# Memory-attention scores as three float32r products in place of one float32 product

## The chip, the cores and the metric

The kernel runs on one core of a Trainium2 chip. The metric is the device time of one execution in microseconds (us), as the median of several runs. Beside it there is one profiled execution, whose trace gives the start and the duration of every instruction on every engine. The engines are called as in the profile: PE (TensorE, matrix products), PEld (its weight loads), DVE (VectorE), ACT (ScalarE), POOL (GpSimd) and SP (SyncE, which here only issues transfers).

## The reference: what is computed

Two layers of an encoder for 256 tokens of width 2048. Each layer makes one wide projection of the normed tokens, splits it among three groups of heads, and projects their joint output back. The group that matters here is the memory attention: 4 heads of 128 columns, whose queries come from the projection and whose keys and values come from 256 memory tokens.

```python
h = rmsnorm(x, norm_g[l])
proj = h @ w_in[l]
a_x, a_b, a_c, a_g, d_q, d_k, d_v, d_g, m_q, m_g = jnp.split(proj, offsets, axis=-1)
# ... group A: gated conv -> y_a ; group D: differential attention, 6 heads -> y_d
mk = rmsnorm(mkv[..., :W_MEM].reshape(b, N_MEM, MEM_HEADS, MEM_HEAD_DIM), mem_k_norm_g[l])
mq = rmsnorm(m_q.reshape(b, s, MEM_HEADS, MEM_HEAD_DIM), mem_q_norm_g[l])
sc = jnp.einsum('bshd,bmhd->bhsm', mq, mk).astype(jnp.float32) * (MEM_HEAD_DIM ** -0.5)
p = jax.nn.softmax(sc, axis=-1)
y_m = jnp.einsum('bhsm,bmhd->bshd', p, mv).reshape(b, s, W_MEM) * jax.nn.silu(m_g)
x = x + jnp.concatenate([y_a, y_d, y_m], axis=-1) @ w_out[l]
```

The change touches the line `sc = ...`, for 4 heads in each of 2 layers: 8 score matrices of 256 queries by 256 memory tokens.

## The kernel before, in words

**Products.** The large projections are made in float32r: every operand `v` is split into a high part `hi` (a copy into a float32r tile, on ACT) and a low part `lo = v - hi` (on DVE), and a product is the sum of three: high by high, high by low, low by high. Lines 301 to 303 are those three, each with a 128x128 stationary operand and 512 moving columns. The weights come from memory in pieces, are split by lines 280 (`hi`) and 281 (`lo`), and each of the tiles `raw`, `hi` and `lo` has four buffers. The scores of the differential heads (lines 541 and 542) are float32r as well, with 256 moving columns. The memory heads' scores (line 587) are one plain float32 product for each 128 queries: `mqT` by `mkT`, two float32 tiles.

**Chunks.** The function `block` walks over the 16 row tiles of a weight matrix two at a time. One such pair is a chunk: it loads and splits the weights, issues 12 products of 512 columns (2 row tiles, 2 token tiles, 3 products), and then calls `run_side`, which advances the side work. Side work is written as Python generators in the list `tasks`: each runs until its next `yield n`, and is due again `n` chunks later. So the order of the program is written by the chunk counter. A block of the projections is 8 chunks.

**A pair of heads.** The generator `pair` takes two heads through scores, softmax, transposes, the weighted sum with the values (line 434, `po`), the output gate, another transpose, and the split of the result into `yT`. Each turn of a matrix goes out to memory and back by eight transfers on the SP queue, four out (line 413) and four back (line 417), two chunks later (`carry`). At most two pairs' `e` tiles are held at once (`held["e"]`). Count the chunks of a layer from the end of the block in which `start` is set (block 4 of the projection), and the memory heads stand like this before the change: the turned queries are issued at chunk 31 and put the layer into `queries`; heads 0 and 1 are scored at 31 and 33, heads 2 and 3 at 39 and 41; the weighted sums stand at 47, 49, 55 and 57, the outward transfers of the outputs at 61 and 69, and the outputs are split into `yT` (lines 252 and 253) at 63, 64, 71 and 72. The output projection begins with chunk 73 and takes the row tiles of the heads first: those of memory heads 2 and 3 (row tiles 14 and 15) in chunk 77.

**What fixes the order.** Instructions wrapped in `keep_in_program_order` (`pin`) stay in the order of the program on their engine. The others, among them lines 280 and 281, all products of the blocks and everything in `mem_scores`, are placed by the planner of the framework, which simulates the program when it is built. Each engine then works through its own list.

**Slots.** `yT` has 32 slots of 128x256 (2 parts by 16 row tiles) per layer. Row tiles 0 to 5 are the conv groups, 6 to 11 the differential heads, 12 to 15 the memory heads. Until the outputs come, the slots are used otherwise: slots 0 to 5 of both parts hold the differential queries, 6 to 11 the first form of the keys, and 12 to 15 (`k_second`) the second form of the keys of differential heads 0 to 3. The set `scored` holds the differential heads whose scores have been issued.

Of the kernel before, what the change touches and what calls it, by code (L numbers as in the profile page):

```python
# [11 lines left out]
F32 = mybir.dt.float32  # L12
F32R = mybir.dt.float32r
I32 = mybir.dt.int32
AF = mybir.ActivationFunctionType
ALU = mybir.AluOpType
# [3 lines left out]
P = 128  # L20
D_MODEL = 2048
SEQ = 256
# [6 lines left out]
CG = W_CONV // P  # L29
DH = W_DIFF // P  # L30
# [18 lines left out]
def encoder(ctx: ExitStack, tc: tile.TileContext, x, mem, norm_g, w_in, conv_w, conv_b,  # L49
            dq_g, dk_g, lq1, lk1, lq2, lk2, head_g, mem_norm_g, w_mem_kv, mq_g, mk_g, w_out, out):  # L50
    nc = tc.nc
    x, mem, out = x[0], mem[0], out[0]

    def pool(name, bufs, space=None):
        kw = {"space": space} if space is not None else {}
        return ctx.enter_context(tc.tile_pool(name=name, bufs=bufs, **kw))
# [6 lines left out]
    small = pool("small", 3)  # L63
# [7 lines left out]
    def nm(s):  # L71
        uid[0] += 1
        return f"{s}_{uid[0]}"
# [131 lines left out]
    def later(g, n):  # L205
        due[id(g)] = chunk[0] + n
        return g
# [200 lines left out]
    def carry(sheet, to):  # L408


        d = dram.tile([NA, B, NA, sheet.shape[-1]], F32, name=nm("d"))
        for a in range(NA):
            tc.keep_in_program_order(nc.sync.dma_start(d[:, :, a].rearrange("b c r -> c b r"), sheet[a * B:(a + 1) * B]))
        yield 2
        of = d.rearrange("b c a (n i) -> (b c) a n i", i=B)
        for a in range(NA):
            tc.keep_in_program_order(nc.sync.dma_start(to[:, :, a], of[:, a]))
# [11 lines left out]
    def weighted(eT, i, v, h):  # L429

        po = ps_t.tile([P, NT, P], F32, tag="t", name=nm("po"))
        for t in range(NT):
            for k in range(NT):
                nc.tensor.matmul(po[:, t, :], eT[:, i, t, k, :], v[:, k, h * P:(h + 1) * P],  # L434
                                 start=k == 0, stop=k == NT - 1)
        return po
# [52 lines left out]
    scored = set()  # L489
# [3 lines left out]
    def pair(heads, begin, end, v):  # L493

        es = []
        for h in heads:
            while held["e"] == 2:
                yield 1
            held["e"] += 1
            es.append((yield from begin(h)))  # L500
            yield 2
        yield 4
        while held["sh"] == 2:
            yield 1
        held["sh"] += 1
        sh = tmp.tile([P, NA, 2, NT * NT, B], F32, tag="sh", name=nm("sh"))
        for i, e in enumerate(es):
            tc.keep_in_program_order(nc.vector.transpose(
                sh[:, :, i], e[0].rearrange("p t (k b c) -> p b (t k) c", k=NT, b=NA)))
            held["e"] -= 1  # L510
            yield 1
        yield 4
        flat = sh.rearrange("p b h n c -> p (b h n c)")
        yield from carry(sh.rearrange("p b h n c -> p b (h n c)"), flat.rearrange("p (n a i) -> p n a i", a=NA, i=B))
        eT = flat.rearrange("p (h t k q) -> p h t k q", h=2, t=NT, k=NT)
        while held["yn"] == 2:
            yield 1
        held["yn"] += 1
        yn = tmp.tile([P, NA, 2, NT, B], F32, tag="yn", name=nm("yn"))
        for i, h in enumerate(heads):  # L520
            end[0](h, yn[:, :, i], weighted(eT, i, v, h), *es[i][1:])
            yield 2
        held["sh"] -= 1
        yield 5
        tc.keep_in_program_order(nc.vector.transpose(yn, yn))
        yield 5
        flat = yn.rearrange("p b h t c -> p (b h t c)")
        yield from carry(yn.rearrange("p b h t c -> p b (h t c)"), flat.rearrange("p (n a i) -> p n a i", a=NA, i=B))
        for i, h in enumerate(heads):
            end[1](h, flat[:, i * SEQ:(i + 1) * SEQ])  # L530
            yield 1
        held["yn"] -= 1
# [45 lines left out]

    queries = set()

    def mem_scores(l, h, qT, kT, st):
        while l not in queries:
            yield 1
        sc = P ** -0.5
        s = ps_s.tile([P, NT, SEQ], F32, tag="s", name=nm("s"))
        for i in range(NT):
            nc.tensor.matmul(s[:, i, :], qT[:, h, i * P:(i + 1) * P], kT[:, h, :], start=True, stop=True)  # L587
        mx = small.tile([P, NT], F32, tag="mmx", name=nm("mmx"))
        nc.vector.tensor_reduce(mx, s, AX.X, ALU.max)
        nc.vector.tensor_scalar(mx, mx, -sc, None, ALU.mult)  # L590
        sm = small.tile([P, NT], F32, tag="msm", name=nm("msm"))
        e = tmp.tile([P, NT, SEQ], F32, tag="e", name=nm("me"))
        for i in range(NT):
            nc.scalar.activation(e[:, i], s[:, i], AF.Exp, bias=mx[:, i:i + 1], scale=sc, accum_out=sm[:, i:i + 1])
        r = small.tile([P, NT], F32, tag="mr", name=nm("mr"), bufs=6)
        nc.vector.reciprocal(r, sm)
        nc.vector.tensor_tensor(r, r, st[:, HR], ALU.mult)
        return e, r

    def mem_out(h, yn, po, r, a):  # L600
        for i in range(NT):
            nc.vector.scalar_tensor_tensor(yn[:, :, i], strips(po[:, i, :]), r[:, i:i + 1],
                                           strips(a[:, i, h * P:(h + 1) * P]), ALU.mult, ALU.mult)
# [25 lines left out]
    def stats_of(parts, tag):  # L629
        ss = small.tile([P, NT], F32, tag="ssum", name=nm("ssum"))  # L630
        nc.vector.tensor_reduce(ss, parts, AX.X, ALU.add)
        return row_stats(ss, tag)

    def T_tile(what):
        kept.append(big.tile([P, 2, KT, SEQ], F32R, tag="T", name=nm(what)))
        return kept[-1]
# [52 lines left out]
    mkT, mv, away, raws, parts = [], [], [], {}, {}  # L689
# [96 lines left out]
    for _ in range(DEPTH):  # L786
        l = len(mkT)
# [38 lines left out]
    for g in range(3, NG):  # L826
        l, k = divmod(g, KT)
# [19 lines left out]
    for l in range(DEPTH):  # L847
        st = stats_of(ssx, "st")
# [5 lines left out]
        yT = T_tile("yT")  # L854
# [5 lines left out]
        def begin_pair(n, p):  # L860
            tasks.append(later(p, max(1, start + PAIR_EVERY * n - chunk[0])))
# [4 lines left out]
        for b in order:  # L866
# [7 lines left out]
            if b == 4:  # L874
                start = chunk[0]
# [18 lines left out]
        mqT = keep.tile([P, MH, SEQ], F32, tag="mqT", name=nm("mqT"))  # L894
# [13 lines left out]
            split_T(yT, CG + DH + h, y, None, pin=True)  # L908

        for n in range(MH // 2):  # L910
            begin_pair(DH // 2 + n, pair((2 * n, 2 * n + 1), lambda h: mem_scores(l, h, mqT, mkT[l], st),
                                         (lambda h, yn, po, r: mem_out(h, yn, po, r, mga), mem_done), mv[l]))


# [80 lines left out]
        for b in range(4):  # L995
# [3 lines left out]
            for t in range(NT):  # L999
                n = 256 if final else NB  # L1000
# [41 lines left out]
```

## Time and profile before

| | |
|---|---|
| time, median of 3 runs | 924.3 us (923.94 to 925.61) |
| profiled execution, its own time | 924.17 us |
| its span, first to last instruction | 922.4 us |
| PE busy | 917.4 us, 99% of the span, 4176 products |
| DVE busy | 669.9 us, 73% |
| ACT busy | 495.0 us, 54% |
| transfers | 215.06 MB, 233 GB/s over the span |
| granted clock of PE | 1.00 |

The span is shorter than the time: some work lies ahead of the first and behind the last instruction. A product in the trace overlaps the next one, so its own duration (379 ns for line 587) is not what it costs; the cost is read from the chain of waits, which lists what each product adds to the time (its pitch). A float32 product of the program is shown as two records: line 587 has 16 products in the program and 32 records.

### The profile page before, as it was taken

How to read it: one execution, taken by the hardware profiler on the slowest of the kernel's cores; microseconds unless marked ns; L12 is line 12 of the kernel's file. 1: busy time of each engine (PE TensorE's matmuls, PEld its weight loads, DVE VectorE, ACT ScalarE, POOL GpSimd, SP SyncE). 2: the span in 40 equal slices, each digit the busy share in tenths (PEclk: the TensorE clock that was granted, in tenths of full speed). 3: DMA queues.
4: the chain of work that ended last, by engine and by line, in shares of the span. 5: the costliest groups of instructions: out<-in, count | busy, mean ns of one | idle time of the engine just before them, and what ended most of it. 6: DMA issues, size and time to landing. Idle time of an engine off the chain costs nothing.

```text
span 922.4 us, 12254 instructions
## 1 busy us (share of the span) xinstructions
PE 917.4 (99%) x4176; PEld 760.6 (82%) x4176; DVE 669.9 (73%) x1179; ACT 495.0 (54%) x754; POOL 7.0 (1%) x18
## 2 busy tenths in 40 slices
PE   9999999999999999999999999999999999999998
PEld 6888888888888888888888888888888888888886
DVE  5797777857898786567676757878898776558652
ACT  6676545675545554445455544568554554446431
POOL 0001000000000000000000000000000000000000
PEclk9999999999999999999999999999999999999999
DMA  8998778876779999988687867886889889988662
GB/s 277 275 275 299 248 229 234 258 206 198 182 214 252 226 267 249 271 244 243 215 264 233 247 188 225 236 236 179 239 229 236 256 213 260 242 239 240 210 220 73
DMA packets 250226, 215.06 MB, mean 233 GB/s; under 512 B 131166, under 2 KB 176820, under 8 KB 250164
## 3 DMA queue, kind: packets, MB, share of 16 engines
q1 hardware_dynamic: 248004, 210.72, 80.0%
q0 software_dynamic: 672, 2.10, 0.6%
q10 hardware_dynamic: 1488, 1.46, 0.5%
q8 instruction: 33, 0.54, 0.2%
q14 instruction: 29, 0.24, 0.1%
HBM read 193.26 MB, written 20.97 MB: 232 GB/s over the span
## 4 chain that ended last, share of the span: by engine, by line
PE 98%; DMA 1%; SPq 0%; DVE 0%; ACT 0%; issue 0%; DVEq 0%
PE acc L301 28%; PE acc L303 28%; PE acc L302 28%; PE acc L735 9%; PE po L434 2%; PE s L587 1%; DMA raw<-in_w_mem_kv_dram 1%; PE s L542 1%; PE s L541 1%; PE pt L713 0%; SPq L699 0%; SPq L693 0%; DVE lo L708 0%; ACT hi L707 0%; DVE xs L1003 0%
## 5 line engine op out<-in xcount | busy, mean ns | idle before, releaser
L280 ACT CAST hi<-raw 128x1024 fp32r<-128x1024 f32 x288 | 302.8, 1052 | 347.0 <-PE acc L303 298.6
L281 DVE TENSOR_TENSOR lo<-raw,hi 128x1024 fp32r<-128x1024 f32 x288 | 351.9, 1223 | 185.4 <-ACT hi L280 180.4
L301 PE MATMUL acc<-hi,xT 128*128 128x512 f32 x896 | 350.2, 392 | 0.0
L302 PE MATMUL acc<-lo,xT 128*128 128x512 f32 x896 | 349.0, 390 | 0.0
L303 PE MATMUL acc<-hi,xT 128*128 128x512 f32 x896 | 348.8, 389 | 0.0
L303 PEld LDWEIGHTS acc<-hi,xT 128*128 128x128 f32 x896 | 168.2, 188 | 35.0
L301 PEld LDWEIGHTS acc<-hi,xT 128*128 128x128 f32 x896 | 168.2, 188 | 34.0
L302 PEld LDWEIGHTS acc<-lo,xT 128*128 128x128 f32 x896 | 168.3, 188 | 33.8
L301 PE MATMUL acc<-hi,yT 128*128 128x512 f32 x256 | 99.6, 389 | 0.0
L302 PE MATMUL acc<-lo,yT 128*128 128x512 f32 x256 | 99.6, 389 | 0.0
L303 PE MATMUL acc<-hi,yT 128*128 128x512 f32 x256 | 99.6, 389 | 0.0
L735 PE MATMUL acc<-hi,memT 128*128 128x512 f32 (+1 forms) x260 | 72.8, 394 | 0.2
L303 PEld LDWEIGHTS acc<-hi,yT 128*128 128x128 f32 x256 | 48.1, 188 | 10.1
L301 PEld LDWEIGHTS acc<-hi,yT 128*128 128x128 f32 x256 | 48.1, 188 | 9.9
L302 PEld LDWEIGHTS acc<-lo,yT 128*128 128x128 f32 x256 | 48.1, 188 | 9.9
L735 PEld LDWEIGHTS acc<-hi,memT 128*128 128x128 f32 x260 | 47.1, 188 | 10.8 <-ACT hi L707 0.8
L708 DVE SCALAR_TENSOR_TENSOR lo<-raw,cva,hi 128x1024 fp32r<-128x1024 f32 (+2 forms) x37 | 41.7, 1137 | 8.8 <-ACT hi L707 7.9
L707 ACT ACTIVATE hi<-raw,cva 128x1024 fp32r<-128x1024 f32 (+2 forms) x37 | 37.6, 1033 | 9.6 <-DMA raw<-in_w_mem_kv_dram 8.1
L735 PE MATMUL acc<-lo,memT 128*128 128x512 f32 (+1 forms) x130 | 39.9, 388 | 0.0
L735 PEld LDWEIGHTS acc<-lo,memT 128*128 128x128 f32 x130 | 24.3, 188 | 5.2
L552 ACT ACTIVATE e<-e,mx 128x256 f32<-128x256 f32 x48 | 23.8, 499 | 1.4 <-DVE mx L548 1.3
L546 DVE SCALAR_TENSOR_TENSOR e<-dist,s 128x512 f32<-128x512 f32 x24 | 15.7, 681 | 2.3 <-PE s L542 1.9
(147 smaller groups left out, 591.3 us busy)
## 6 DMA issues: line engine op xcount, KB each, us to landing
raw<-in_w_in_dram SPq DMA_DIRECT2D x192, 512.0 KB, 4.4
raw<-in_w_out_dram SPq DMA_DIRECT2D x64, 512.0 KB, 4.2
raw<-in_w_in_dram SPq DMA_DIRECT2D x64, 256.0 KB, 4.6
raw<-in_w_mem_kv_dram SPq DMA_DIRECT2D x30, 512.0 KB, 4.0
d<-sh SPq DMA_DIRECT2D x80, 128.0 KB, 3.9
sh<-d SPq DMA_DIRECT2D x64, 128.0 KB, 4.9
d<-yn SPq DMA_DIRECT2D x40, 64.0 KB, 3.6
yn<-d SPq DMA_DIRECT2D x40, 64.0 KB, 4.2
```

Source lines behind the costliest of these rows:

```text
L280: nc.scalar.copy(hi, raw)
L281: nc.vector.tensor_tensor(lo_, raw, hi.bitcast(F32), ALU.subtract)
L301: nc.tensor.matmul(acc[t], sh, hi, start=first, stop=False)
L302: nc.tensor.matmul(acc[t], sh, lo, start=False, stop=False)
L303: nc.tensor.matmul(acc[t], sl, hi, start=False, stop=last)
L434: nc.tensor.matmul(po[:, t, :], eT[:, i, t, k, :], v[:, k, h * P:(h + 1) * P], start=k == 0, stop=k == NT - 1)
L541: nc.tensor.matmul(s[c][:, i, :], qi, k_first(yT, c, h), start=True, stop=False)
L546: nc.vector.scalar_tensor_tensor(e[:, c], dist, -slopes[h], s[c], ALU.mult, ALU.add)
L552: nc.scalar.activation(e[:, c, i], e[:, c, i], AF.Exp, bias=mx[:, c, i:i + 1], accum_out=sm[:, c, i:i + 1])
L707: pin(nc.scalar.activation(hi, raw, AF.Copy, scale=gain))
L708: pin(nc.vector.scalar_tensor_tensor(lo, raw, gain, hi.bitcast(F32), ALU.mult, ALU.subtract))
L735: pin(nc.tensor.matmul(accs[l, half][t][:, at:at + n], memT[:, token_part, k, t * P:(t + 1) * P], p, start=k == 0 and at == 0 and token_pa ...
```

## The change

For every memory head, query and key are split into a high and a low part, as the other operands are, and the score is the sum of three float32r products of 256 columns. The parts of the key stand in a new tile `mkp` of one buffer; those of the query stand in slots 12 to 15 of `yT`, the ones that the outputs of the same heads take later. Since differential keys stand there before, the scores now wait until all six differential heads are in `scored`. Between the splits and the products there is a `yield 1`.

```diff
-    def mem_scores(l, h, qT, kT, st):
-        while l not in queries:
+    def mem_scores(l, h, yT, qT, kT, st):
+        while l not in queries or not all((l, d) in scored for d in range(DH)):
             yield 1
         sc = P ** -0.5
+        q = yT[:, :, CG + DH + h, :]
+        k = small.tile([P, 2, SEQ], F32R, tag="mkp", name=nm("mkp"), bufs=1)
+        for parts, of in ((k, kT), (q, qT)):
+            nc.scalar.copy(parts[:, 0], of[:, h, :])
+            nc.vector.tensor_tensor(parts[:, 1], of[:, h, :], parts[:, 0].bitcast(F32), ALU.subtract)
+        yield 1
         s = ps_s.tile([P, NT, SEQ], F32, tag="s", name=nm("s"))
         for i in range(NT):
-            nc.tensor.matmul(s[:, i, :], qT[:, h, i * P:(i + 1) * P], kT[:, h, :], start=True, stop=True)
+            for q_part, k_part in ((0, 0), (0, 1), (1, 0)):
+                nc.tensor.matmul(s[:, i, :], q[:, q_part, i * P:(i + 1) * P], k[:, k_part],
+                                 start=q_part + k_part == 0, stop=q_part == 1)
...
-            begin_pair(DH // 2 + n, pair((2 * n, 2 * n + 1), lambda h: mem_scores(l, h, mqT, mkT[l], st),
+            begin_pair(DH // 2 + n, pair((2 * n, 2 * n + 1), lambda h: mem_scores(l, h, yT, mqT, mkT[l], st),
```

## The prediction

> **What bounds the kernel now.** I read the head of the profile page first: the span, the busy time of PE, its slices, the granted clock, and the chain of waits by engine and by line.
>
> ```profile
> span 922.4 us, 12254 instructions
> ...
> PE 917.4 (99%) x4176; PEld 760.6 (82%) x4176; DVE 669.9 (73%) x1179; ACT 495.0 (54%) x754; POOL 7.0 (1%) x18
> ...
> PE   9999999999999999999999999999999999999998
> ...
> PEclk9999999999999999999999999999999999999999
> ...
> PE 98%; DMA 1%; SPq 0%; DVE 0%; ACT 0%; issue 0%; DVEq 0%
> PE acc L301 28%; PE acc L303 28%; PE acc L302 28%; PE acc L735 9%; PE po L434 2%; PE s L587 1%; DMA raw<-in_w_mem_kv_dram 1%; PE s L542 1%; PE s L541 1%; PE pt L713 0%; SPq L699 0%; SPq L693 0%; DVE lo L708 0%; ACT hi L707 0%; DVE xs L1003 0%
> ```
>
> PE sets the end: the chain that ended last is PE for 98% of the span, and PE is busy in every slice at a granted clock of full speed. So whatever PE no longer does comes off the time, and work of the other engines costs nothing until PE has to wait for it. Line 587, the scores that change, is 1% of the chain. PE and PEld have the same count, so every product has its own weight load; nothing is saved by two products in a row with the same stationary operand.
>
> Next I read the pitch of the products from the chain of waits in order of time (start, us added, what). First a stretch of nothing but 512-column products, 31 of them between the two rows; then one memory head of before; then one differential head, whose 8 products of lines 541 and 542 have the shape and type that the change gives to the memory heads.
>
> ```profile
> 416.95 0.23 PE acc L301
> ...
> 423.98 0.23 PE acc L302
> ```
>
> ```profile
> 300.16 0.23 PE acc L303
> 300.39 0.87 PE s L587 x4
> 301.26 0.23 PE acc L301
> ```
>
> ```profile
> 264.02 0.12 PE s L541
> ...
> 264.84 0.12 PE s L542
> 264.96 0.24 PE acc L301
> ```
>
> The 512-column product costs (423.98 - 416.95) / 31 = 0.2268 us. A memory head costs 0.87 us, in four records (two float32 products). The float32r products of 256 columns cost (264.96 - 264.02) / 8 = 0.1175 us each. The groups of PE's instructions, kept apart by shape, show the two shapes and how many records there are of the old one:
>
> ```profile
> L541 PE MATMUL s<-yT 128*128 128x256 f32 x48 | 12.3, 286 | 0.0
> ...
> L587 PE MATMUL s<-mkT,mqT 128*128 128x256 f32 x32 | 8.2, 379 | 0.0
> ```
>
> **PE's part of the change.** Removed: 32 records, four for each of 8 heads, 8 x 0.87 = 6.96 us. Added: 2 x 3 products for each of 8 heads, 48 x 0.1175 = 5.64 us. Both stand on the chain, so the difference does too: -1.32 us. The price of a product has bounds. From below, half of the 512-column pitch, 0.1134 us, gives -1.52 us. From above, the 0.12 us of the single rows gives 48 x 0.12 = 5.76, so -1.20 us. I take -1.3 us, since the row of 8 is the same shape in the same kind of place.
>
> [...]
>
> **ACT's and DVE's part.** Added for each head are two copies to float32r of 128x256 on ACT and two subtractions of that shape on DVE. The profile has both for the memory outputs:
>
> ```profile
> L252 ACT CAST yT<-yn 128x256 fp32r<-128x256 f32 x8 | 3.2, 402 | 0.0
> ```
>
> ```profile
> L253 DVE TENSOR_TENSOR yT<-yn,yT 128x256 fp32r<-128x256 f32 x8 | 3.3, 414 | 0.0
> ```
>
> That makes 16 x 0.402 = 6.4 us on ACT and 16 x 0.414 = 6.6 us on DVE over the kernel, in five windows where the memory heads are scored and softened:
>
> ```profile
> core 0: us, PE busy (x) PEld busy (x) DVE busy (x) ACT busy (x) POOL busy (x), PEclk, DMA share, GB/s
> 300.00:325.00 25.00, 25.00 (x120) 21.01 (x119) 18.68 (x42) 13.72 (x29) 0.00 (x0) 1.00 0.92 237
> 325.00:350.00 25.00, 25.00 (x115) 20.84 (x114) 18.59 (x47) 12.69 (x22) 0.00 (x0) 1.00 0.93 246
> 690.00:715.00 25.00, 25.00 (x120) 21.00 (x119) 21.70 (x72) 11.74 (x22) 0.00 (x0) 1.00 0.96 230
> 715.00:740.00 25.00, 25.00 (x120) 21.02 (x119) 18.00 (x45) 12.77 (x28) 0.00 (x0) 1.00 0.88 249
> 740.00:765.00 25.00, 25.00 (x116) 20.82 (x115) 18.31 (x40) 13.40 (x22) 0.00 (x0) 1.00 0.83 206
> ```
>
> DVE, the busier one, has 3.3 us or more free in each 25 us, and a pair of heads adds 4 x 0.414 = 1.7 us to it. Covered by that, I cost this work at nothing; if the cover were gone, 6.6 us would be the most that it could add.
>
> **The order's part: waits.** The new instructions stand in the lists of ACT and DVE ahead of weight parts that PE needs, so what counts is how far ahead these run. The tightest place that I found is the first pair of layer 0. ACT's list there, DVE's next low part, and PE's chain at the end of chunks 33 and 36:
>
> ```profile
> 300.43 1.05 ACT L280 CAST hi<-raw 128x1024 fp32r<-128x1024 f32 x1 [0.85 <-PE acc L303]
> ...
> 304.64 1.04 ACT L280 CAST hi<-raw 128x1024 fp32r<-128x1024 f32 x1
> ...
> 309.56 0.91 ACT L255 ACTIVATE yT<-yn,hgain 128x256 fp32r<-128x256 f32 x2 [2.96 <-DMA yn<-d]
> 310.37 1.03 ACT L280 CAST hi<-raw 128x1024 fp32r<-128x1024 f32 x1
> ```
>
> ```profile
> 311.57 1.22 DVE L281 TENSOR_TENSOR lo<-raw,hi 128x1024 fp32r<-128x1024 f32 x1
> ```
>
> ```profile
> 306.51 0.23 PE acc L303
> ...
> 315.58 0.23 PE acc L303
> 315.82 0.89 PE po L434 x8
> ```
>
> With four buffers the high part of chunk 35 starts at 300.43, when PE has ended chunk 31 (300.39); so 304.64 is chunk 36 and 310.37 chunk 37. ACT stood for 2.96 us in front of it, waiting for a transfer of the differential outputs. The low part of chunk 37 is ready at 311.57 + 1.22 = 312.8, and PE, which ends chunk 36 at 315.8 and then has 0.89 us of line 434, needs it at 316.7: a lead of 3.9 us. Two copies and two subtractions ahead of it, one after the other, take 1.6 us. 2.3 us remain, so no stall follows from the work alone.
>
> The query's copy also waits for the turned queries. Their four transfers stand on the SP queue so, and land after the time in the second row:
>
> ```profile
> 287.76 4.15 SPq L417 DMA_DIRECT2D mqT<-d  x4
> ```
>
> ```profile
> DMA to landing us min/median/max: 4.3/4.5/4.8
> ```
>
> The last one lands at about 287.76 + 4.15 + 4.5 = 296.4; the four operations end by about 298 or 299, and the products, now at the end of chunk 32, come at 300.39 + 2.72 = 303.1. The condition on `scored` costs nothing: the last differential head is issued at chunk 21, ten chunks earlier.
>
> A new wait is the single buffer of `mkp`: the second head's key copy needs the first head's products done. Counted through the generators, the first pair's parts stand at chunks 31 and 34 and the products at 32 and 35. Between the two scores lie three chunks, 3 x 12 x 0.2268 = 8.2 us, less 0.7 for the products themselves; the splits need 1.6. The copy should find the buffer free or nearly so, if nothing else stands before it.
>
> **The order's part: later outputs.** With one more chunk per head, the first pair is 2 chunks later and the second pair, which waits for `e` tiles at 41 instead of 39, is 4 later: the outputs of heads 2 and 3 are split at chunks 75 and 76, no longer 71 and 72, and are needed in chunk 77. The program order holds by one chunk. In time, layer 0 and then layer 1, the last split's subtraction and the first product of the output projection (chunk 73):
>
> ```profile
> L253 DVE TENSOR_TENSOR yT<-yn,yT x4: 381/418/419, 387.9 to 412.4; 128x256 fp32r<-128x256 f32 x4
> ```
>
> ```profile
> 420.87 0.39 PE L301 MATMUL acc<-hi,yT 128*128 128x512 f32 x1
> ```
>
> ```profile
> L253 DVE TENSOR_TENSOR yT<-yn,yT x3: 417/418/419, 801.0 to 825.5; 128x256 fp32r<-128x256 f32 x3
> ```
>
> ```profile
> 831.19 0.39 PE L301 MATMUL acc<-hi,yT 128*128 128x512 f32 x1
> ```
>
> Chunk 77 begins four chunks (4 x 2.72 = 10.9 us) behind chunk 73, at 431.8 and 842.1. The last split ends at 412.8 and 825.9; four chunks later that is 423.7 and 836.8. So 8.1 and 5.3 us of slack remain. What else moves are the eight transfers of that pair's outputs on the SP queue, now at chunks 73 and 75, beside the conv group's own. In layer 1 the SP queue shows those, out and back, as:
>
> ```profile
> 820.54 1.96 SPq L413 DMA_DIRECT2D d<-sh  x4
> ...
> 826.06 4.89 SPq L417 DMA_DIRECT2D uT<-d  x4
> ```
>
> Four outward transfers take 1.96 us of SP, less than the slack, and the outputs' own four are two chunks apart from their way back. I cost it at nothing; if it ate the slack, the output projection would stall.
>
> **The sum.** The profiled execution took 924.17 us, 1.8 of it outside the span of 922.4. 924.17 - 1.3 = 922.9. The median shown is 0.13 us above this execution, so I forecast 923.0 us, 0.14% less. What a measurement of this kernel can tell from no change is about 0.2%, 1.85 us: the three runs before spread by 1.7 us.
>
> **The rivals.**
> [...]
> *The one buffer stalls PE (slower).* If the second head's key copy stands in ACT's list behind a wait like that at 309.56, the four operations start at about 310.4 and, with two subtractions for the outputs and a row maximum between them on DVE, end near 313.2. PE reaches the products at 300.39 + 4 x 2.72 + 0.7 = 312.0, so it stands for 1.2 us. At all four second heads that is 4.8 us: 924.3 - 1.3 + 4.8 = 927.8. It cancels the gain from 0.33 us per second head on, and is told from no change from 0.8 us on. For it speaks that ACT's next high part did start only behind that wait. [...] Against it: the other three places show no such wait, and the copies are placed by the planner, which can put them ahead.
> *The late heads stall the output projection.* In layer 1 the slack is 5.3 us; 1.96 us of SP for the conv group's transfers and 4.89 for its way back, if both came ahead of the outputs' transfers, overdraw it by 1.6 us: 924.6. Against it: the way back stands two chunks later in the program, and lines 413 and 417 are pinned.
> *DVE becomes the bound.* All 6.6 us on the path: 929.6. Against it stand the free shares above.
> *No gain beyond the noise, with another sign.* The planner places everything behind the first scores anew; a shift of a microsecond either way can't be excluded, and widens the forecast's own range.
>
> **How the numbers follow.** The forecast 0.78, the full quarter 0.05, the one buffer 0.08, the late heads 0.05, DVE 0.04. The bound of faster by 0.2% lies at 922.45, only 0.55 us below the forecast, which is a third of the spread of the runs: of the 0.78 I put 0.16 there and 0.62 within 0.2%; the full quarter is split 0.02 and 0.03; the one buffer 0.03 same and 0.05 slower, the late heads 0.03 and 0.02, DVE 0.04 slower. Sums: faster 0.18, same 0.71, slower 0.11. The range goes from 922.0 (the full quarter and half a microsecond of scatter) to 924.9 (the late heads' price and a little scatter).
>
> **What would show it.** In the changed kernel's chain of waits, six records of the new score line should add 0.70 us where four added 0.87, eight times. PE's idle time ahead of them and ahead of the products behind them should stay 0.0. If PE waits for the parts at the second head of a pair, the one buffer is right; if the output projection's products wait for row tile 14 or 15, the late heads are; if line 281 is what PE waits for, DVE is. The forecast is wrong if the span differs from 921.1 us by more than a microsecond, or if the new products' pitch is not between 0.113 and 0.12.

## The result, and the profile after

The changed kernel takes **922.85 us** (median of 21 runs, 922.41 to 924.33), the kernel before 924.2 us (median of 21 runs, 923.43 to 926.27). The ratio is 0.9986, with a 95% interval of 0.998 to 0.9992: a gain of 0.14%, inside the 0.2% that the prediction called no change. The profiled execution took 922.70 us with a span of 920.9, 0.2 us from the 921.1 that the prediction named.

The head of the profile page of the changed kernel:

```profile
span 920.9 us, 12319 instructions
...
PE 915.9 (99%) x4192; PEld 761.0 (83%) x4192; DVE 671.9 (73%) x1195; ACT 501.9 (54%) x770; POOL 7.0 (1%) x18
...
PE 99%; DVE 0%; DVEq 0%; issue 0%
PE acc L303 28%; PE acc L301 28%; PE acc L302 28%; PE acc L743 10%; PE po L434 2%; PE s L542 1%; PE s L541 1%; PE s L594 1%; PE pt L721 0%; PE warm L122 0%; DVE xs L1011 0%; DVEq L1045 0%; PE pva L811 0%; PE pvb L142 0%
```

PE still sets the end, with 16 records more (48 new ones for 32 old ones) and 1.5 us less of busy time. The new score line, 594, is still 1% of the chain.

The chain of waits in order of time (start, us added, what), around the first two memory heads of layer 0 and the last one of layer 1:

```profile
302.64 0.23 PE acc L303
302.87 0.70 PE s L594 x6
303.57 0.23 PE acc L301
...
311.53 0.23 PE acc L303
311.76 0.70 PE s L594 x6
...
751.82 0.70 PE s L594 x6
```

Six records add 0.70 us, 0.117 each, at all eight heads; four added 0.87 before. From 303.57 to 311.76 PE's chain goes on without a gap: between the two heads lie three chunks, as the generators say, and 8.19 us.

The beginning of layer 0 and the end of the kernel, in the kernel before and then in the changed one. Of each, first PE's first product of layer 0 (start, duration), then the last sum of line 1003 or 1011 in the chain:

```profile
97.62 0.39 PE L301 MATMUL acc<-hi,xT 128*128 128x512 f32 x1
```

```profile
918.42 0.42 DVE xs L1003
```

```profile
97.39 0.39 PE L301 MATMUL acc<-hi,xT 128*128 128x512 f32 x1
```

```profile
916.72 0.42 DVE xs L1011
```

From the first product of layer 0 to the start of the last sum, the kernel before takes 918.42 - 97.62 = 820.80 us and the changed one 916.72 - 97.39 = 819.33: **1.47 us less**. By the same marks, the first product with `yT` (the start of the output projection) splits it into 0.74 us in layer 0, 0.74 in layer 1 and nothing behind. I call this stretch the later stretch, and what lies ahead of it the beginning. Where PE doesn't wait in it, the later stretch turned out to be the sharpest measure that the traces give, and the experiments are read by it as well as by their times.

The splits, in ACT's and DVE's lists of layer 0 (start, duration, what, idle time ahead of it and what ended that):

```profile
294.61 1.33 ACT L588 CAST yT<-mqT 128x256 fp32r<-128x256 f32 x4 [1.90 <-DMA mqT<-d]
...
304.43 0.41 ACT L588 CAST mkp<-mkT 128x256 fp32r<-128x256 f32 x1
```

```profile
295.04 1.10 DVE L589 TENSOR_TENSOR yT<-mqT,yT 128x256 fp32r<-128x256 f32 x3 [0.18 <-ACT yT L588]
...
296.20 0.42 DVE L589 TENSOR_TENSOR yT<-mqT,yT 128x256 fp32r<-128x256 f32 x1
...
306.90 0.41 DVE L589 TENSOR_TENSOR mkp<-mkT,mkp 128x256 fp32r<-128x256 f32 x1
```

The four query copies of a layer stand together behind the landing of the turned queries, for which ACT waited 1.90 us. The second head's key copy starts 0.86 us behind the first head's last product (303.57), and its subtraction ends at 307.3, 4.5 us ahead of the second head's products.

### The profile page after: what moved, and what is told of

Same layout as the page of the kernel before. It is cut to its first block, busy times and chain, and to the rows that moved or that the text cites. A ratio compares the mean times of both kernels' runs of the same rounds, so it can differ in the third digit from the quotient of the medians.

```text
span 920.9 us, 12319 instructions
## 1 busy us (share of the span) xinstructions
PE 915.9 (99%) x4192; PEld 761.0 (83%) x4192; DVE 671.9 (73%) x1195; ACT 501.9 (54%) x770; POOL 7.0 (1%) x18
## 4 chain that ended last, share of the span: by engine, by line
PE 99%; DVE 0%; DVEq 0%; issue 0%
PE acc L303 28%; PE acc L301 28%; PE acc L302 28%; PE acc L743 10%; PE po L434 2%; PE s L542 1%; PE s L541 1%; PE s L594 1%; PE pt L721 0%; PE warm L122 0%; DVE xs L1011 0%; DVEq L1045 0%; PE pva L811 0%; PE pvb L142 0%
```

## The experiments

Every kernel below is the changed kernel with one edit. The ratio is to the kernel before, run on the same chip, with its 95% interval. The later stretch is from one trace of each kernel.

| kernel | median, us | ratio | later stretch, us | beginning, us |
|---|---|---|---|---|
| before | 924.2 | | 820.80 | 97.62 |
| changed | 922.85 | 0.9986 (0.998 to 0.9992) | 819.33 | 97.39 |
| changed, again | 922.79 | 0.9983 (0.9974 to 0.9992) | 819.33 | 97.27 |
| splits, float32 product | 924.19 | 1.0005 (0.9996 to 1.0014) | 820.83 | 97.33 |
| one product | 919.05 | 0.9946 (0.9934 to 0.9959) | 815.60 | 97.63 |
| four products | 924.89 | 1.0009 (1.0 to 1.0018) | 821.41 | 97.49 |
| products of 128 columns | 927.47 | 1.0033 (1.0021 to 1.0046) | 824.35 | 97.71 |
| key's parts in `yT` | 923.57 | 0.9994 (0.9986 to 1.0003) | 819.51 | 98.77 |
| the same again | 923.33 | 0.9985 (0.9976 to 0.9994) | 819.51 | 97.42 |
| splits pinned | 923.18 | 0.9987 (0.9978 to 0.9996) | 819.33 | 98.83 |
| no pause | 923.14 | 0.9986 (0.9977 to 0.9995) | 819.52 | 97.62 |
| pause of two chunks | 922.82 | 0.9985 (0.9976 to 0.9994) | 819.34 | 97.23 |
| five splits | 925.09 | 1.0009 (1.0 to 1.0017) | 822.79 | 98.84 |
| five splits, key's parts in `yT` | 923.81 | 0.9991 (0.9982 to 1.0) | 821.71 | 97.48 |

### Where the gain comes from

**The splits and the order alone.** The score is again one float32 product; all that the change adds beside PE stays.

```diff
-            for q_part, k_part in ((0, 0), (0, 1), (1, 0)):
-                nc.tensor.matmul(s[:, i, :], q[:, q_part, i * P:(i + 1) * P], k[:, k_part],
-                                 start=q_part + k_part == 0, stop=q_part == 1)
+            nc.tensor.matmul(s[:, i, :], qT[:, h, i * P:(i + 1) * P], kT[:, h, :], start=True, stop=True)
```

> The splits, the wait for the differential heads and the extra chunk stay; the score is one float32 product again, so the parts are made and not read. Theory (only PE's pitch moves the time, the splits are covered): no gain and no loss, 924.2 us, ratio 1.000, within 0.1%. Rival (the splits and the later order cost something that the cheaper products hide): slower than the kernel before by what they cost, at most the 6.6 us that all the subtractions take on DVE, 924.2 to 930.8 us.

Measured: 924.19 us, ratio 1.0005 (0.9996 to 1.0014), and a later stretch of 820.83 us, 0.03 from the kernel before's. The chain has the old price in the new place:

```profile
302.82 0.87 PE s L593 x4
```

So the work of the splits, the wait for the differential heads and the extra chunks cost nothing that can be measured, and nothing of the gain comes from a new placing of the rest. PE doesn't read the parts here, and the planner put the key copies early (101.0 to 144.7 us), so this run doesn't tell whether PE waits for the parts; that it doesn't is seen in the changed kernel's own trace, where PE waits for nothing in the later stretch.

**One product.**

```diff
-            for q_part, k_part in ((0, 0), (0, 1), (1, 0)):
-                nc.tensor.matmul(s[:, i, :], q[:, q_part, i * P:(i + 1) * P], k[:, k_part],
-                                 start=q_part + k_part == 0, stop=q_part == 1)
+            nc.tensor.matmul(s[:, i, :], q[:, 0, i * P:(i + 1) * P], k[:, 0], start=True, stop=True)
```

> Only the product of the high parts is made; the two with a low part are left out, so the scores have the precision of one float32r product. Theory (each product adds its pitch, 0.1175 us, to the time): 32 products less than the changed kernel, 32 x 0.1175 = 3.76 us, so 922.85 - 3.76 = 919.1 us, ratio to the kernel before 0.9945. Rival (a quarter of the float32 pitch, 0.109 us): 919.4 us. Rival (a part of the gain comes from elsewhere, as a new placing by the planner): further than 1 us from 919.1.

Measured: 919.05 us, against an expected 919.1. The later stretch is 3.73 us shorter than the changed kernel's, 3.73 / 32 = 0.1166 us for each product left out.

**Four products.**

```diff
-            for q_part, k_part in ((0, 0), (0, 1), (1, 0)):
+            for q_part, k_part in ((0, 0), (0, 1), (1, 0), (1, 1)):
                 nc.tensor.matmul(s[:, i, :], q[:, q_part, i * P:(i + 1) * P], k[:, k_part],
-                                 start=q_part + k_part == 0, stop=q_part == 1)
+                                 start=q_part + k_part == 0, stop=q_part + k_part == 2)
```

> The product of the two low parts is added, so four float32r products stand where one float32 product stood. Theory (0.1175 us each on the path): 16 products more, +1.88 us, 922.85 + 1.88 = 924.7 us, ratio to the kernel before 1.0006. If four float32r products cost what the float32 product costs (0.109 us each): 924.2 us by the kernel before's own price, ratio 1.000.

Measured: 924.89 us, against an expected 924.7, and a later stretch 2.08 us longer than the changed kernel's; 1.88 were expected of the pitch alone. Layer 1 has 0.94 of it, as the pitch gives, and layer 0 has 1.14. The 0.20 beyond stands at one weighted sum of layer 0, which adds 1.09 us where 0.89 is usual; its weight loads start late (PEld's one wait ahead of line 434 in this trace is 0.3 us of issue), and why isn't shown:

```profile
316.00 1.09 PE po L434 x8
```

Four float32r products are dearer than the float32 product in whose place they stand: the chains of this kernel and of the one-product kernel show 8 records in 0.93 us, where the float32 product has 0.87, and 2 in 0.23.

```profile
302.98 0.93 PE s L594 x8
```

```profile
303.11 0.23 PE s L593 x2
```

With one, three and four products in place, the time goes by their number at about 0.117 us each. Together with the kernel that keeps the float32 product, that settles the source of the gain.

**Products of 128 columns.** The same sums in twice as many products of half the width.

```diff
-            for q_part, k_part in ((0, 0), (0, 1), (1, 0)):
-                nc.tensor.matmul(s[:, i, :], q[:, q_part, i * P:(i + 1) * P], k[:, k_part],
-                                 start=q_part + k_part == 0, stop=q_part == 1)
+            for c in range(0, SEQ, P):
+                for q_part, k_part in ((0, 0), (0, 1), (1, 0)):
+                    nc.tensor.matmul(s[:, i, c:c + P], q[:, q_part, i * P:(i + 1) * P], k[:, k_part, c:c + P],
+                                     start=q_part + k_part == 0, stop=q_part == 1)
```

> Each float32r product of 256 columns is cut into two of 128 columns: 12 products for each head, the same sums. If a product costs by its columns alone, twelve at 0.059 us take 0.70 us, and nothing changes: 922.85 us. If a product can't be shorter than the load of its weights, bounded by the 0.111 us of the 128-column float32 records of line 434, twelve take 1.33 us and the time rises by 8 x 0.63 = 5.0 us: 927.9 us. I expect the second, or a little under it, 926 to 928.

Measured: 927.47 us, ratio 1.0033 (1.0021 to 1.0046), in the range of the second case. Twelve records add 1.29 us:

```profile
302.97 0.23 PE acc L303
303.19 1.29 PE s L595 x12
304.48 0.28 PE acc L301
304.76 0.23 PE acc L302
```

The row of twelve isn't their whole price, since the product behind it adds 0.28 us where 0.23 is usual. By the later stretch, 5.02 us over the changed kernel's, the 96 products of 128 columns cost (48 x 0.1166 + 5.02) / 96 = 0.111 us each, against 0.117 for one of 256: half the columns save a twentieth. It is also the 0.111 of the 128-column float32 records of line 434, from which the expectation took its bound. The weight loads of these products are, in the trace:

```profile
L595 PEld LDWEIGHTS s<-mkp,yT x96: 187/192/192, 302.8 to 757.5; 128*128 128x128 f32 x96
```

A record takes 192 ns at the median, longer than the 0.111 us that one product costs; the first starts at 302.8, where twelve of them one after the other would take 12 x 0.192 = 2.30 us, and the row of twelve products ends at 304.48, so they overlap. That the load of the weights bounds the price was my assumption: the runs show the price, not what sets it.

### What the waits could have cost

**The key's parts in `yT`.** The one-buffer tile goes; each memory head's key parts stand in the slot of a differential query that has been used.

```diff
-        k = small.tile([P, 2, SEQ], F32R, tag="mkp", name=nm("mkp"), bufs=1)
+        k = yT[:, :, h, :]
```

> The key's parts stand in the slots of yT that held the differential queries of heads 0 to 3, each memory head in its own, so the one-buffer tile and its wait are gone. Theory (the wait is covered, PE never stood for it): the same as the changed kernel, 922.85 us, ratio to the kernel before 0.9986, within 0.05%. Rival (the one buffer costs PE something at the second heads): faster than the changed kernel by at least 0.3 us for each of four second heads, 921.6 us or less.

The first run left this open: 923.57 us, ratio 0.9994 (0.9986 to 1.0003), slower than the changed kernel instead of equal or faster. The trace said where: the later stretch was 819.51 us, 0.18 over the changed kernel's, and the rest of it lay in the beginning, 98.77 us instead of 97.39, where the lists of PE, ACT and DVE are the same in both. So I ran it again.

> The kernel with the key's parts in yT again. In its first trace everything from the first product of layer 0 on took 819.51 us, the changed kernel 819.33; the stretch ahead took 98.77 us, the changed kernel 97.39 and 97.27. Theory (the beginning is scatter): near 922.9 us now, ratio to the kernel before near 0.9985, and the later stretch again 819.3 to 819.6. Rival (the key's place costs time): 923.5 us again, with the loss in the later stretch.

Measured: 923.33 us, ratio 0.9985 (0.9976 to 0.9994), beginning 97.42, later stretch 819.51 again. Ahead of that run, the changed kernel itself had gone a second time:

> The changed kernel as it is, beside the others on their chip, and with a second trace. From the first product of layer 0 to the last one (L301 of the projection to the last L1011), both layers should take what the first trace shows, 916.72 - 97.39 = 819.3 us, within 0.2 us; the stretch ahead of it, 97.39 us there and 98.77 us in the kernel with the key's parts in yT, may differ from trace to trace. If that stretch is again near 97.4 us here and the median 0.7 us under the other's, the key's place does something to the beginning; if it varies, the beginning is scatter.

Measured: 922.79 us, ratio 0.9983 (0.9974 to 0.9992), beginning 97.27, later stretch 819.33 again. By the condition set there, this alone spoke for the key's place: the beginning was near 97.4 again, and the median 0.78 us under the 923.57. The second run above decided against it, since the kernel with the key's parts in `yT` began once in 98.77 us and once in 97.42. So the beginning is scatter, and taking the one buffer away gains nothing: the later stretch is 0.18 us longer in both traces.

**The splits pinned.** The planner may no longer move them.

```diff
-            nc.scalar.copy(parts[:, 0], of[:, h, :])
-            nc.vector.tensor_tensor(parts[:, 1], of[:, h, :], parts[:, 0].bitcast(F32), ALU.subtract)
+            pin(nc.scalar.copy(parts[:, 0], of[:, h, :]))
+            pin(nc.vector.tensor_tensor(parts[:, 1], of[:, h, :], parts[:, 0].bitcast(F32), ALU.subtract))
```

> The splits keep the place that the program gives them on ACT and DVE, so the planner can't put the four query copies of a layer together nor the key's copy ahead. Theory of the prediction's rival (the one buffer stalls PE if the copy stands behind a wait): up to 1.2 us at each of four second heads, 924 to 927.7 us. My theory now (the key's copy starts 0.9 us behind the first head's products and has 8 us until its own): no stall, 922.85 us, later stretch 819.3 to 819.8 us.

Measured: 923.18 us, ratio 0.9987 (0.9978 to 0.9996), later stretch 819.33, the same to 0.01 us; in it PE waits for nothing. So the planner's freedom isn't what hides the splits either.

**No pause, and a longer one.** The first kernel drops the `yield 1` behind the splits, the second makes it `yield 2`.

```diff
-        yield 1
         s = ps_s.tile([P, NT, SEQ], F32, tag="s", name=nm("s"))
```

> The pause of one chunk between splits and products is gone; the memory heads stand where they stood before the change, and the splits directly ahead of their products. Theory (ACT and DVE run ahead of PE by enough, and the planner places the splits early anyway): the same as the changed kernel, 922.85 us, later stretch 819.3 us. Rival (without the pause PE stands for the four operations, 1.6 us, at some of the 8 heads): up to 8 x 1.6 = 13 us more; 0.5 us at each second head would show as 924.9.

Measured: 923.14 us, ratio 0.9986 (0.9977 to 0.9995), later stretch 819.52, and no wait of PE in it. The pause isn't needed.

```diff
-        yield 1
+        yield 2
         s = ps_s.tile([P, NT, SEQ], F32, tag="s", name=nm("s"))
```

> The pause between splits and products is two chunks, no longer one. Counted through the generators, the last outputs are then split at chunk 79 and 80, behind chunk 77 which needs them, so the program forces the side work forward there, in both layers. Theory (the late heads have a point from which they decide: 7.1 us of slack in the trace of the changed kernel, 10.9 us for four chunks more): PE waits for row tile 14 or 15, 10.9 - 7.1 = 3.8 us in each layer at most, less what the forcing takes back: 923 to 930.5 us, most likely 926. Rival (the planner hides that too): 922.85 us as the changed kernel.

Measured: 922.82 us, ratio 0.9985 (0.9976 to 0.9994), later stretch 819.34; the 926 us that I held most likely didn't come. The last output is late all the same: the subtractions that split the outputs in layer 0, in the changed kernel and then in this one, are

```profile
L253 DVE TENSOR_TENSOR yT<-yn,yT x2: 382/400/419, 419.6 to 423.3; 128x256 fp32r<-128x256 f32 x2
```

```profile
L253 DVE TENSOR_TENSOR yT<-yn,yT x3: 418/418/419, 401.5 to 438.2; 128x256 fp32r<-128x256 f32 x3
```

so the last one, row tile 15, ends at 438.6. In the program's order the chunk of row tiles 14 and 15 begins four chunks, 10.9 us, behind 419.74, at 430.6, and its second half, row tile 15, at 432.0: the output is 6.6 us late. PE didn't wait, because the planner put other products there. Of each product of the output projection the first of its three (line 301) in PE's list, from the fourth piece of weights on, in this kernel (with the tile numbers of the built program, which the trace leaves out):

```
acc_3965<-hi_4028   acc_3966<-hi_4028   acc_3965<-hi_4028   acc_3966<-hi_4028
acc_4132<-hi_4136   acc_4133<-hi_4136   acc_4132<-hi_4136   acc_4133<-hi_4136
acc_4132<-hi_4154   acc_4133<-hi_4154
acc_3965<-hi_4048   acc_3966<-hi_4048   (row tile 14)
acc_4132<-hi_4154   acc_4133<-hi_4154   acc_4132<-hi_4172   acc_4133<-hi_4172
acc_4132<-hi_4172   acc_4133<-hi_4172   acc_4132<-hi_4190   acc_4133<-hi_4190
acc_3965<-hi_4048   acc_3966<-hi_4048   (row tile 15)
```

`hi_4048` is the fifth piece, for row tiles 14 and 15; the accumulators 4132 and 4133 belong to the second block of the output projection, which needs row tiles 6 to 13 first. In the changed kernel the fifth piece follows the fourth at once. Counted through that list, row tile 15 is first read by the 33rd product of line 301 with `yT`, 2.9 us behind the end of its split:

```profile
441.50 0.39 PE L301 MATMUL acc<-hi,yT 128*128 128x512 f32 x1
```

**Five splits.** Each split is made five times, to find out how much cover there is.

```diff
-        for parts, of in ((k, kT), (q, qT)):
+        for parts, of in ((k, kT), (q, qT)) * 5:
```

> Each split is made five times over, with the same result, so 64 copies more on ACT (25.7 us) and 64 subtractions more on DVE (26.8 us) stand where the memory heads are scored. Theory (the splits lie in free time: DVE had 3.3 to 7.0 us of 25 free in the five windows, some 30 us in all): between no change and a loss of about 3 us, 922.85 to 926. Rival (the work of the splits counts in part): a loss of half of DVE's time or more, 936 us or more.

Measured: 925.09 us, ratio 1.0009 (1.0 to 1.0017); the later stretch is 822.79, 3.46 us over the changed kernel's, 3.34 of it in layer 0. The traced execution, 927.38 us, was the longest of the eleven; by the medians of the same chip the loss is 925.09 - 922.79 = 2.30 us. The beginnings of all traces differ by 1.6 us at most, and these eleven runs by 2.85, so in this kernel the later stretch isn't the same in every execution. PE and PEld waited in the later stretch for (us in total, times, longest):

```profile
PEld s L594 <- ACT mkp L588: 1.8, 1, 1.8
PEld po L434 <- issue: 1.7, 1, 1.7
```

```profile
PE s L594 <- ACT mkp L588: 1.4, 1, 1.4
PE po L434 <- DMA sh<-d: 1.3, 1, 1.3
```

The copy of the first wait is the last of the five for the second head of a pair. In ACT's list it stands behind a differential output that waited for its transfer, as the prediction's rival of the one buffer had it:

```profile
357.79 0.51 ACT L255 ACTIVATE yT<-yn,hgain 128x256 fp32r<-128x256 f32 x1 [3.86 <-DMA yn<-d]
358.20 0.67 ACT L423 ACTIVATE th<-acc,st 128x512 f32<-128x512 f32 x1
358.77 0.39 ACT L588 CAST mkp<-mkT 128x256 fp32r<-128x256 f32 x1
```

**Five splits without the buffer.** The same, with the key's parts in `yT`.

```diff
-        k = small.tile([P, 2, SEQ], F32R, tag="mkp", name=nm("mkp"), bufs=1)
+        k = yT[:, :, h, :]
...
-        for parts, of in ((k, kT), (q, qT)):
+        for parts, of in ((k, kT), (q, qT)) * 5:
```

> Each split five times over, as in the earlier run that took 925.09 us, but with the key's parts in yT, so no head waits for another's. Theory (there PE waited 1.4 and 1.8 us for key copies that stood behind the one buffer, not for want of time on DVE): 922.9 to 923.5 us, later stretch under 820 us. Rival (the work of DVE itself is too much there): 925 us, later stretch near 822.8 us again.

Measured: 923.81 us, ratio 0.9991 (0.9982 to 1.0), later stretch 821.71: between the two cases. This trace too is of a long execution, 924.94 us, the second longest of eleven; by the medians of the same chip, the five splits cost 923.81 - 923.33 = 0.48 us over the kernel with the key's parts in `yT`. In the traces, layer 0 is 2.20 us over the changed kernel's instead of 3.34. The waits left are

```profile
PEld po L434 <- issue: 1.6, 1, 1.6
PEld s L594 <- DVE yT L589: 0.5, 1, 0.5
PEld s L594 <- ACT yT L588: 0.4, 1, 0.4
```

```profile
PE po L434 <- DMA sh<-d: 1.2, 1, 1.2
```

So at five times the work the one buffer costs 1.08 us by the two traces and 1.28 by the two medians, as a net difference of two kernels whose other waits differ as well; what share of the loss it has, these numbers leave open. The waits that remain are for work that comes late: a weighted sum of line 434 waits for a transposed sheet, and two score products for late splits. With each split made once, none of them is there.

No kernel here beats the changed one by more than the scatter, but for the one that leaves out two of the three products.

## Why the prediction was right, point by point

**The price of the products** was the whole result. Forecast: 0.1175 us each and -1.32 us in all, from eight products of a differential head. Measured: 0.117 in the chain, 8 x (0.87 - 0.70) = 1.36 us by the rows and 1.47 by the later stretch; the rows are rounded to 0.01 us, which allows 1.28 to 1.44, and the rest isn't assigned. That the median came within 0.15 us of the 923.0 is in part luck: the medians of the kernel before, in four groups of 21 to 33 runs, lie between 923.98 and 924.33. The full quarter in the prediction's chances and range (0.87 / 8 = 0.109 us for a new product, 922.6 us in all) is a price that no run shows: the chains have 0.70 / 6 = 0.117 us in the changed kernel and 0.93 / 8 = 0.116 with four products; the median alone couldn't tell 922.6 from 923.0. By the rows, three float32r products cost 0.70 / 0.87 = 0.80 of the float32 product.

**The cover** was right: costed at nothing, and 0.03 us in the kernel that keeps the splits and the old product. The price of the work was right too (copies 0.402 us, subtractions 0.418 against a forecast 0.414). Its limit was not worked out in the prediction: the free shares of DVE (3.3 us and more of each 25) left room for more, but five times the work did stall PE, by 3.46 us in the traced execution and 2.30 by the medians, for 26.8 us of repeated subtractions on DVE and 25.7 us of repeated copies on ACT.

**The order of the splits** was wrong in its place, though not in its effect. The step read "the first pair's parts stand at chunks 31 and 34", as counted through the generators. The splits aren't pinned, and the planner put the four query splits of a layer together, at 294.61 us, and the first key split as early as 101.8, beside the keys' own work. When they were pinned to the places that I had counted, the later stretch was the same. The landing of the queries, estimated at 296.4, came at 294.6.

**The one buffer** cost nothing, as the forecast had it: in the later stretch of the changed kernel PE waited for nothing; the rival's 4.8 us would have needed all four second heads behind a wait like the one at 309.56, and with the splits pinned or without the pause PE waited for none of them. What the rival had right is the mechanism: at five times the work a second head's key copy did stand behind such a wait, of 3.86 us, and PE stood for the copy.

**The late heads.** The times of the last splits were forecast at 423.7 and 836.8 us, with 8.1 and 5.3 us of slack. Layer 0's subtractions of the changed kernel stand above, with the kernel of the longer pause. Here are the start of its output projection in layer 0, then layer 1's subtractions and start:

```profile
419.90 0.39 PE L301 MATMUL acc<-hi,yT 128*128 128x512 f32 x1
```

```profile
L253 DVE TENSOR_TENSOR yT<-yn,yT x4: 384/418/419, 803.1 to 832.9; 128x256 fp32r<-128x256 f32 x4
```

```profile
829.48 0.39 PE L301 MATMUL acc<-hi,yT 128*128 128x512 f32 x1
```

They end at 423.7 and 833.3; chunk 77 begins at 430.8 and 840.4, so the slack is 7.1 us in both layers. In layer 1 the last split moved by 7.4 us (825.9 to 833.3), not by the 10.9 of four chunks that the forecast had; why is not shown. The step that failed stands behind that: "if it ate the slack, the output projection would stall". With the pause of two chunks it did eat the slack, with an output 6.6 us late, and nothing stalled, because products aren't pinned. Slack against the program's order is no price when the planner owns the order.

**The range and the scatter.** I had put 0.16 on a measured gain of more than 0.2% because the runs before spread by 1.7 us. The runs do spread so; their medians lie within 0.35 us in the four larger groups, and the later stretch of the changed kernel was the same in both its traces.

## What to carry to other kernels

Where PE sets the end, a product is priced by its pitch in a row of its own kind in the same trace, with what it leaves to the product behind it: here three float32r products of 256 columns (0.117 us each) beat one float32 product (0.435), and four lose. At 128 columns the same exchange would lose already, as I estimate from the prices here (it wasn't run), since three float32r products at 0.111 us (0.33) stand against the 0.222 of two float32 records of line 434; so look at the number of moving columns before splitting operands. And if a planner orders the work, a wait that was counted from the program's text is only a place to look at: test it by pinning the work, by lengthening the pause, or by repeating the work until it shows.

## What the runs showed of the hardware that I had not expected

Behind the first product of layer 0, where PE doesn't wait, the traces repeat to a hundredth of a microsecond: 819.33 in both traces of the changed kernel, 819.51 in both of the one with the key's parts in `yT`, and 87.23 or 87.24 us from the start of the second output projection to the start of the last sum in all fourteen traces. The five splits are the exception, as their runs show above. Most of the scatter of the profiled executions lies in the first 100 us, which took 97.2 to 98.8 us, with the same lists of work on PE, ACT and DVE; what follows the start of the last sum took 3.9 to 4.2 us, and 4.8 once (splits, float32 product). Two of the three traces with 98.8 (the key's parts in `yT` once, and the pinned splits) have no fast product among the first ones, the 256-column products of line 743; the third (five splits) has, but PE stood for a token part instead. Line 743 in the trace of the pinned splits and in the second one of the changed kernel (shortest, median and longest duration in ns), then the wait in the trace of the five splits:

```profile
L743 PE MATMUL acc<-hi,memT x260: 387/390/628, 5.3 to 98.1; 128*128 128x512 f32 x126, 128*128 128x256 f32 x4
```

```profile
L743 PE MATMUL acc<-hi,memT x260: 278/389/582, 5.0 to 96.6; 128*128 128x512 f32 x126, 128*128 128x256 f32 x4
```

```profile
PEld acc L743 <- ACT memT L252: 1.4, 1, 1.4
```

The first twelve products of line 743, of 256 columns, take 2.72 us in the trace of the pinned splits (5.32 to 8.04) and 1.72 in the other (5.05 to 6.77), so 1.0 of the 1.56 us between the two beginnings lies there; the granted clock is shown as 1.00 in both. What makes a beginning slow wasn't tried and stays open. For small changes without waits of PE, the stretch behind the beginning, taken from a single trace, told a difference of 0.2 us that eleven runs of a kernel didn't.
